# A hybrid decoder layer on one core: the list schedule's reserve for TensorE's operands becomes a preference, and the kept weights get another layout

## The chip, the cores and the metric

The kernel runs on one core of one Trainium2 chip. The metric is the device time of one execution in microseconds. The program is built once by a Python script: the script lists all operations of the layer, a list scheduler in the script decides in which order each engine gets them, and each engine then works through its own queue in that fixed order, waiting on semaphores where an operand is not there yet. The engines are TensorE (PE, with its weight loads PEld), VectorE (DVE), ScalarE (ACT), GpSimd (POOL) and SyncE (SP), which issues nearly all DMAs.

## The reference

One decoder layer for 2048 tokens of width 1024, in float32. An input `x` is normalized and modulated, multiplied by one wide input matrix (columns gq, gk, gv, ga, gz for gated linear attention, sq, sk, sv, sz for sliding window attention), goes through the two kinds of attention, then through one output matrix, and is normalized again:

```python
h = rmsnorm(x, g_norm) * (1 + scale) + shift
proj = einsum('bsd,de->bse', h, w_in)
gq, gk, gv, ga, gz, sq, sk, sv, sz = split_cols(proj, COL_SIZES)
o_gla = rmsnorm(gla_chunked(gq, gk, gv, log_sigmoid(ga @ w_decay + b_decay) / 16), g_head) * silu(gz)
o_swa = sliding_window_sink_attention(rope(sq), rope(sk), sv, sinks) * silu(sz)
x = x + gate * (concat([o_gla, o_swa]) @ w_out)
return rmsnorm(x, g_final)
```

## The kernel before, in words

**Tiling.** The 2048 tokens are four units (`u` = 0 to 3) of 512. For each unit the input product is made slot by slot: a slot is a group of columns (`qk0`, `gz0`, `sz0`, `qk1`, `gz1`, `sz1`, `kv`, `sq`, `gv`). Each float32 operand is split into a high part rounded to a format that TensorE takes in one pass and a low part, the rest. A product is then three: high by high, high by low, low by high (`mm3`). So in the rows `hh`, `hl` are the two parts of the normalized input (eight tiles, one for each 128 of the 1024 rows of the matrix, counted by `k`), and `w_sz`, `w_gz`, `w_kv` and so on hold both parts of a slot's weights.

**Weights.** In unit 0 each raw weight tile (`wr_...`) comes by DMA from the input, ACT rounds it to the high part (CAST), and DVE or POOL subtracts for the low part. Both parts are then stored to a buffer in the chip's memory (`wc`), and units 1 to 3 load them from there. The slots `qk0`, `gz0`, `sz0` of unit 0 are made first, together, `k` by `k`, while the input is still being normalized (`first_w`, `proj_t_outer`; products `po`). Their weights lie in the tiles `first` (qk0) and `own` (gz0 and sz0, one pair for each `k`).

**Buffers.** Weight tiles of all slots share five buffers (`WB`): the two `first` tiles, then `w_sz_0`, `w_gz_0` and `w_kv_0`. The sixth tile, `w_kv_1`, takes the buffer of the first `first` tile, `w_kv_2` that of the second, `w_kv_3` that of `w_sz_0`, and the tiles of the next slot that of `w_gz_0`. A tile can only be written when its buffer's former content has been read by TensorE and stored to `wc`. Products of a slot go to one of two PSUM banks (tag `mm`) and are evacuated by ACT (`zs`, `kvr`); a third product tile needs the first one evacuated. Raw tiles take turns in three buffers (`st`) or four (`wst`); the four lie in memory which the start of unit 0 uses until its last `hl` is made.

**Order.** `Order.issue` holds a model of the engines. At each step it takes the engine that can begin earliest, and on it, among the operations whose operands the model has ready, the one with the lowest key (the program's order, with lifts). For an operation of TensorE an operand counts as ready 0.9 in the model's clock (`SLACK`) after its producer has ended and the semaphore has hopped over: `after()`, line 303. If no operation of TensorE is ready by that measure, the model lets TensorE stand until one is. Nothing of these 0.9 is in the program itself: only the order that comes out is. A store to `wc` has its key raised by 400 or more, so that it comes late on SP.

Of the kernel before, what the change touches and what calls it, by code (L numbers as in the profile page):

```python
# [18 lines left out]
P = 128  # L19
# [76 lines left out]
class Order:  # L96
# [122 lines left out]
    def issue(self):  # L219
# [14 lines left out]
        for g in units:  # L234
            inside = {o.idx for o in g}
            deps = {d for o in g for d in o.deps if d.idx not in inside}
            ready = 0.0
            pending = set()
            for d in deps:
                if d.start is None:  # L240
                    pending.add(unit_of[d.idx])
                else:
                    ready = max(ready, self.after(d, g[0]))
            need[g[0].idx] = [len(pending), ready, g, deps]
            for p in pending:
                users.setdefault(p, []).append(g[0].idx)
# [13 lines left out]
        for k, (n, ready, g, _) in need.items():  # L260
            if n == 0:
                avail[g[0].eng].append([ready, g[0].key, k])
        left = len(units)
        out = []
        while left:
# [36 lines left out]

    def after(self, d, o):
# [89 lines left out]
def layer_kernel(ctx, tc, x, xT, w_ada, w_gate, b_cols, b_gate, g_cols, c_cols, pos, inv_freq,  # L393
# [30 lines left out]
    def f(ap):  # L424
        return ap.bitcast(F32)
# [239 lines left out]
    def first_w():  # L665


        n = SLOT_N["qk0"]
        t0 = [w_tile(f"w{i}_first").rearrange("p (k n) -> p k n", n=n) for i in "hl"]
        t1 = [[hp.tile([P, 2, n], F32R, name=f"w{'hl'[i]}_own{k}", tag="hh" if i == 0 else "hl")  # L670
               if k < KT - 2 else
               near.tile([P, 2, n], F32R, name=f"w{'hl'[i]}_own{k}", tag=f"qk{i}" if k == KT - 2 else "zs",
                         bufs=2 if k == KT - 2 else ZS)
               for k in range(KT)] for i in range(2)]
        src = w_in[:, 0:3 * KT * n].rearrange("p (k n) -> p k n", n=3 * n)
        raws = {}

        def load(k):
            raws[k] = begin.tile([P, 3, n], F32, name=f"wr_first{k}", tag="st0", bufs=3)
            SY.dma_start(raws[k].rearrange("p a b -> p (a b)"), src[:, k])  # L680

        def part(k):
            raw = raws.pop(k)
            both = ([t[:, k] for t in t0], raw[:, 0]), ([t[k] for t in t1], raw[:, 1:3])
            for d, r in both:
                (G.tensor_copy if k == 0 else A.copy)(d[0], r)
            for d, r in both:
                G.tensor_tensor(d[1], r, f(d[0]), ALU.subtract)
            if k == 0:
                for i in range(2):  # L690
                    keep_k(i, 0)

        def keep_k(i, k, lift=None):
            o = 2 * SLOT_O["gz0"]
            to = wc[:, o:o + 4 * KT * n].rearrange("p (s c i k m) -> p s c i k m", s=2, c=2, i=2, k=KT)
            od.lift = LATER if lift is None else lift
            x = SY.dma_start(f(to[:, :, :, i, k]), f(t1[i][k]).rearrange("p s (c m) -> p s c m", c=2))
            od.lift = 0
            return x

        def keep_parts(after):
            ops = [keep_k(i, k, 0) for k in (KT - 1, KT - 2) for i in range(2)]
            o = 2 * SLOT_O["qk0"]
            to = wc[:, o:o + 2 * KT * n].rearrange("p (c i k m) -> p c i k m", c=2, i=2, k=KT)
            for i in range(2):
                for c in range(2):
                    ops.append(SY.dma_start(f(to[:, c, i]), f(t0[i][:, :, c * P:(c + 1) * P])))
            for x in ops:
                x.deps.add(after)

        def keep_rest():
            after = od.ops[-1]
            for i in range(2):
                for k in range(1, KT - 2):
                    keep_k(i, k, 0).deps.add(after)

        parts = [[[t0[i][:, k] for k in range(KT)] for i in range(2)]]
        for j in range(2):
            parts.append([[t1[i][k][:, j] for k in range(KT)] for i in range(2)])
        return parts, load, part, keep_parts, keep_rest  # L720
# [13 lines left out]
    def slot_w(u, name, lift=LIFT):  # L734
# [7 lines left out]
        tiles = {}  # L742
        kept = wc[:, 2 * o:2 * (o + KT * n)].rearrange("p (j i k m) -> p j i k m", j=count, i=2, k=kk)
        src = w_in[:, o:o + KT * n].rearrange("p (j k m) -> p j k m", j=count, k=kk)
        step = max(1, NB // m)

        def load(j):
            t = w_tile(f"w_{name}{u}_{j}")[:, :2 * kk * m].rearrange("p (i k m) -> p i k m", i=2, k=kk)
            tiles[j] = t
            od.lift = -lift  # L750
            if u == 0:
                for k in range(0, kk, step):
# [5 lines left out]
                    raw = raw[:, :step * m].rearrange("p (k m) -> p k m", k=step)  # L758
                    h_, l_ = [t[:, i, k:k + step] for i in range(2)]
                    SY.dma_start(raw, src[:, j, k:k + step])  # L760
# [4 lines left out]
            else:  # L765
                for k in range(0, kk, kk // 2):
                    SY.dma_start(f(t[:, :, k:k + kk // 2]), f(kept[:, j, :, k:k + kk // 2]))

        stream.extend([lambda j=j: load(j) for j in ([int(half)] if half else range(count))])

        def w(i, k, c=0):
            return tiles[k // 2][:, i, k % 2] if wide else tiles[c][:, i, k]

# [169 lines left out]
    def proj_t_outer(ws, each):  # L943
# [5 lines left out]
        for k in range(KT):  # L949
            each(k)  # L950
            for h in halves(k):
                for i, w in enumerate(ws):
                    for ct in range(2):
                        cs = slice(ct * P, (ct + 1) * P)
                        p = ps[2 * i + ct]

                        for n, (a, b) in enumerate(((w[0], hh), (w[1], hh), (w[0], hl))):
                            mmul(p[:, h], a[k][:, cs], b[k][:, h], k == 0 and h.start == 0 and n == 0,
                                 k == KT - 1 and n == 2, p)
# [618 lines left out]
```

## Time and profile before

| | |
|---|---|
| three timed runs | 835.5, 836.94, 837.18 us, median 836.94 |
| profiled execution: device time | 835.71 us |
| profiled execution: span from first to last instruction | 834.0 us |
| TensorE busy | 809.6 us, 97% of the span |
| DVE, ACT, POOL busy | 72%, 61%, 47% |
| granted clock of TensorE, mean | 0.997 |
| DMA | 200.81 MB, 118812 packets, queue of SP 68.8% of 16 engines |

Times in the rows are counted from the start of the span. An idle time stands in square brackets before the instruction that ended it, with the instruction or DMA that released it. A busy TensorE is modelled from the start and size of its products; the distance from one product's start to the next shows the rate at which they really follow each other.

### The profile page before, as it was taken

The numbers are of one execution on the slowest core, as the hardware profiler recorded it, in microseconds if no ns is written. First come the engines' busy times: TensorE is split into PE (matmuls) and PEld (weight loads), VectorE is DVE, ScalarE is ACT, GpSimd is POOL, SyncE is SP. The second block draws the span as 40 slices with busy tenths as digits, with TensorE's granted clock in tenths as the row PEclk, the third lists the DMA queues.
The fourth block names the chain that finished last, engine by engine and source line by source line (L and its number), as shares of the span: only waits on it lengthen the run. The fifth ranks groups of instructions, "written<-read, shape, count | busy, mean of one in ns | idle before, by whom it ended". The sixth has DMA issues, their size and how long they took to land.

```text
span 834.0 us, 13255 instructions
## 1 busy us (share of the span) xinstructions
PE 809.6 (97%) x4274; PEld 671.9 (81%) x4274; DVE 597.4 (72%) x1140; ACT 511.0 (61%) x1271; POOL 396.0 (47%) x461
## 2 busy tenths in 40 slices
PE   7998999999999999999999999999999999999995
PEld 6777788879888787888878888888888888888884
DVE  6986567678568978785797747524675766889895
ACT  4567865898556778675587857524677633344431
POOL 4512225456632558645667544322462514665642
PEclk9999999999999999999999999999999999999998
DMA  9969997847448499598887938637467864454432
GB/s 339 377 196 354 388 357 297 288 150 267 174 169 286 142 370 332 180 327 307 284 296 271 380 117 301 219 111 267 143 209 265 288 216 166 141 162 152 140 101 101
DMA packets 118812, 200.81 MB, mean 241 GB/s; under 512 B 10275, under 2 KB 42070, under 8 KB 116054
## 3 DMA queue, kind: packets, MB, share of 16 engines
q1 hardware_dynamic: 117734, 199.91, 68.8%
q8 instruction: 34, 0.56, 0.3%
q14 instruction: 36, 0.29, 0.1%
q10 hardware_dynamic: 1008, 0.05, 0.1%
HBM read 145.26 MB, written 54.66 MB: 240 GB/s over the span
## 4 chain that ended last, share of the span: by engine, by line
PE 67%; DVE 3%; ACT 2%; DMA 2%; POOL 2%; issue 1%; DVEq 0%; ACTq 0%; POOLq 0%
PE pt L439 18%; PE pn L439 17%; PE ya L439 10%; PE ys L439 9%; PE ppo L439 3%; PE psc L439 2%; PE po L439 2%; DMA xt<-in_xT 1%; PE ppt L444 1%; PE pc L439 1%; DMA xn<-in_x 1%; PE pms L439 1%; PE pu L439 1%; ACT s L387 1%; DVE hl L387 1%
## 5 line engine op out<-in xcount | busy, mean ns | idle before, releaser
L439 PE MATMUL pn<-w_gv,hh 128*128 128x512 f32 x256 | 85.6, 398 | 0.0
L439 PE MATMUL pn<-w_sq,hh 128*128 128x512 f32 x256 | 82.0, 395 | 0.0
L439 PE MATMUL pt<-hh,w_gz 128*128 128x512 f32 x224 | 74.8, 397 | 0.1
L439 PE MATMUL pt<-hh,w_qk 128*128 128x512 f32 x224 | 74.9, 399 | 0.0
L439 PE MATMUL pt<-hh,w_sz 128*128 128x512 f32 x224 | 72.8, 394 | 0.2 <-ACT hh L387 0.2
L387 POOL TENSOR_TENSOR y<-u,y 128x512 f32<-128x512 f32 x28 | 42.4, 1518 | 56.7 <-DVE y L387 33.3
L387 ACT ACTIVATE ge<-ge 128x512 f32<-128x512 f32 x96 | 60.6, 631 | 11.3 <-DVE ge L387 10.0
L387 ACT ACTIVATE s<-s,nm 128x129 f32<-128x129 f32 x128 | 51.4, 402 | 19.5 <-DVE nm L387 18.9
L387 POOL TENSOR_TENSOR xt<-xt,rstd 128x512 f32<-128x512 f32 x27 | 38.5, 1433 | 41.1 <-DMA xt<-in_xT 25.6
L439 PE MATMUL pn<-w_kv,hh 128*128 128x272 f32 x256 | 51.1, 292 | 5.1 <-ACT zs L387 1.8
L439 PEld LDWEIGHTS pn<-w_sq,hh 128*128 128x128 f32 x256 | 47.5, 188 | 10.5 <-issue 0.5
L439 PEld LDWEIGHTS pn<-w_gv,hh 128*128 128x128 f32 x256 | 47.1, 188 | 8.6
L439 PE MATMUL ys<-woht,m 128*128 128x512 f32 x168 | 53.4, 392 | 0.0
L439 PE MATMUL pn<-w_gv,hl 128*128 128x512 f32 x128 | 50.4, 394 | 0.0
L439 PE MATMUL pn<-w_sq,hl 128*128 128x512 f32 x128 | 50.3, 393 | 0.0
L387 POOL TENSOR_TENSOR s<-s,den 128x512 f32<-128x512 f32 x32 | 35.2, 1103 | 30.8 <-DVE den L387 24.1
L439 PE MATMUL ya<-wohb,m 128*128 128x512 f32 x152 | 49.6, 392 | 0.0
L439 PEld LDWEIGHTS pt<-hh,w_sz 128*128 128x128 f32 x224 | 41.9, 188 | 9.1 <-ACT hh L387 0.5
L387 POOL TENSOR_TENSOR o<-o,zs 128x128 f32<-128x128 f32 x64 | 34.4, 558 | 31.0 <-DVE o L387 25.5
L439 PEld LDWEIGHTS pt<-hh,w_gz 128*128 128x128 f32 x224 | 41.6, 188 | 9.0 <-DVE w_gz L387 0.6
L387 ACT CAST m<-mr 128x512 fp32r<-128x512 f32 x39 | 23.1, 618 | 41.9 <-PE ya L439 20.7
L439 PEld LDWEIGHTS pt<-hh,w_qk 128*128 128x128 f32 x224 | 41.6, 188 | 7.9
(272 smaller groups left out, 2388.2 us busy)
## 6 DMA issues: line engine op xcount, KB each, us to landing
w_sz<-wc SPq DMA_DIRECT2D x24, 512.0 KB, 6.4
w_sq<-wc SPq DMA_DIRECT2D x24, 512.0 KB, 7.6
w_qk<-wc SPq DMA_DIRECT2D x24, 512.0 KB, 7.0
w_gv<-wc SPq DMA_DIRECT2D x24, 512.0 KB, 8.6
w_gz<-wc SPq DMA_DIRECT2D x24, 512.0 KB, 6.5
mr<-mixd SPq DMA_DIRECT2D x32, 256.0 KB, 3.0
y<-in_x SPq DMA_DIRECT2D x32, 256.0 KB, 3.4
out<-y SPq DMA_DIRECT2D x32, 256.0 KB, 2.2
```

Source lines behind the costliest of these rows:

```text
L387: return order.add(eng, lambda: real(*args, **kw), dur, ins, outs, lock=lock, nbytes=nbytes)
L439: return od.add("PE", lambda: T.matmul(o, l, r, start=start, stop=stop), dur, [l, r] + ([] if start else [o]), [bank if start and bank is ...
L444: return od.add("PE", lambda: T.transpose(o, i, ident), 0.109, [i, ident], [o], mode="few" if o.shape[0] <= 32 else None)
```

## The change

Two edits are made. The first is in the scheduler: for an operation of TensorE an operand now counts as ready as soon as its producer has ended and the hop is over (`HARD` = 0). The old measure with 0.9 added is kept as a second number, `soft`. Among the operations that are ready, the model picks by key among those whose `soft` time has passed; if there are none, it takes the one whose `soft` time comes first. So TensorE never stands in the model while anything can begin.

The second is the layout of the weights in their tiles and in `wc`. Before, all high parts of a tile came first and then all low parts; now high and low alternate for each 128 (or, in wide slots, 272 or 512) columns. A reload of half a tile is then one run of 4096 bytes a partition (`kv`: 2176) where it was two of 2048 (1088). The `own` tiles hold one slot each with both parts, stored in runs of 1024 bytes (512 before); a `first` tile holds both parts of four `k`, stored in runs of 4096 (512 before). To fill them, ACT's and POOL's operations on each raw tile of `first_w` become three of 256 columns each where there were two, of 256 and 512.

```diff
+HARD = 0.0
+WEIGH = 0.0
...
-            pick = min((x for x in lst if when(x, e) <= t + 1e-9), key=lambda x: x[1])
+            now = [x for x in lst if when(x, e) <= t + 1e-9]
+            safe = [x for x in now if x[3] <= t + 1e-9]
+            pick = min(safe, key=lambda x: x[1]) if safe else min(now, key=lambda x: (x[3] + WEIGH * x[1], x[1]))
...
                     ready = max(self.after(d, first) for d in x[3])
-                    avail[first.eng].append([max(ready, x[1]), first.key, u])
+                    soft = max(self.after(d, first, True) for d in x[3])
+                    avail[first.eng].append([ready, first.key, u, soft])
...
-        return d.end + HOP[o.eng] + (SLACK if o.eng == "PE" else SPARE if d.eng == "G" else 0.0) + (PATIENT if o.late and d.bytes else 0.0)
+        t = d.end + HOP[o.eng] + (PATIENT if o.late and d.bytes else 0.0)
+        if o.eng == "PE":
+            return t + (SLACK if soft else HARD)
+        return t + (SPARE if d.eng == "G" else 0.0)
...
         def part(k):
             raw = raws.pop(k)
-            both = ([t[:, k] for t in t0], raw[:, 0]), ([t[k] for t in t1], raw[:, 1:3])
-            for d, r in both:
-                (G.tensor_copy if k == 0 else A.copy)(d[0], r)
-            for d, r in both:
-                G.tensor_tensor(d[1], r, f(d[0]), ALU.subtract)
+            homes = [t0[k // half][:, :, k % half]] + t1[k]
+            for j, t in enumerate(homes):
+                (G.tensor_copy if k == 0 else A.copy)(t[:, :, 0], raw[:, j])
+            for j, t in enumerate(homes):
+                G.tensor_tensor(t[:, :, 1], raw[:, j], f(t[:, :, 0]), ALU.subtract)
...
-                    ops.append(SY.dma_start(f(to[:, c, i]), f(t0[i][:, :, c * P:(c + 1) * P])))
+                    ops.append(SY.dma_start(f(kept(0)[:, c, i * half:(i + 1) * half]), f(t0[i][:, c])))
...
-            t = w_tile(f"w_{name}{u}_{j}")[:, :2 * kk * m].rearrange("p (i k m) -> p i k m", i=2, k=kk)
+            t = w_tile(f"w_{name}{u}_{j}")[:, :2 * kk * m].rearrange("p (k i m) -> p k i m", i=2, k=kk)
...
-                    SY.dma_start(f(t[:, :, k:k + kk // 2]), f(kept[:, j, :, k:k + kk // 2]))
+                    SY.dma_start(f(t[:, k:k + kk // 2]), f(kept[:, j, k:k + kk // 2]))
```

On TensorE the order differs, against the kernel before, from the start to 234 us of the old trace and from 350 to 490 us; elsewhere it is the same. The number of products is the same.

**First place: SP's queue in unit 0, where the weights of slot `kv` are fetched.** Before, behind the first two stores of `own` tiles (the second half of `w_gz_0`, `wr_gz_04`, follows much later, behind the stores of the `first` tiles):

```order
L387 DMA wr_gz_00_187<-in_w_in 128x512
L387 DMA wc<-wh_own_129 128x4x128
L387 DMA wc<-wl_own_137 128x4x128
L387 DMA wr_kv_00_201<-in_w_in 128x272
L387 DMA wr_kv_01_202<-in_w_in 128x272
L387 DMA wr_kv_10_204<-in_w_in 128x272
L387 DMA wr_kv_30_231<-in_w_in 128x272
...
L387 DMA wc<-wl_first 128x8x128 x2
L387 DMA wr_gz_04_188<-in_w_in 128x512
L387 DMA wc<-w_sz_0_183 128x2048
```

Now:

```order
L389 DMA wr_gz_00_187<-in_w_in 128x512
L389 DMA wc<-w_own_129 128x2x256
L389 DMA wc<-w_own_130 128x2x256
L389 DMA wr_gz_04_188<-in_w_in 128x512
L389 DMA wr_kv_11_205<-in_w_in 128x272
L389 DMA wc<-w_sz_0_183 128x2048
...
L389 DMA wr_kv_00_201<-in_w_in 128x272
L389 DMA wr_kv_01_202<-in_w_in 128x272
...
L389 DMA wc<-w_first_127 128x1024 x2
L389 DMA wc<-w_first_128 128x1024
```

The second half of `gz` and the store of `w_sz_0` have moved from behind the stores of the `first` tiles to ahead of them, and ahead of the loads into `w_kv_0`.

**Second place: ACT's queue at the same point of the program.** `zs<-pt_229` and `zs<-pt_235` empty the PSUM banks of the slots `sz1` and `gz1`; the casts make the high parts of the `kv` weights. Before:

```order
L387 CAST w_kv_1_203<-wr_kv_10_204 128x272
L387 CAST w_kv_1_203<-wr_kv_11_205 128x272
L387 COPY zs<-pt_229 128x512
L387 ACTIVATE ge<-ge 128x512
L387 CAST w_kv_2_206<-wr_kv_20_207 128x272
L387 CAST w_gz_0_186<-wr_gz_04_188 128x512
L387 ACTIVATE ge<-ge 128x512 x3
L387 CAST w_kv_3_230<-wr_kv_30_231 128x272
L387 CAST w_kv_3_230<-wr_kv_31_232 128x272
L387 COPY zs<-pt_235 128x512
```

Now:

```order
L389 CAST w_kv_3_230<-wr_kv_30_231 128x272
L389 COPY zs<-pt_229 128x512
L389 ACTIVATE ge<-ge 128x512
L389 CAST w_kv_1_203<-wr_kv_10_204 128x272
L389 CAST w_kv_1_203<-wr_kv_11_205 128x272
L389 ACTIVATE ge<-ge 128x512
L389 CAST w_kv_3_230<-wr_kv_31_232 128x272
L389 ACTIVATE ge<-ge 128x512 x2
L389 COPY zs<-pt_235 128x512
L389 CAST w_kv_2_206<-wr_kv_20_207 128x272
L389 CAST w_kv_2_206<-wr_kv_21_208 128x272
```

`zs<-pt_229` no longer stands behind the casts into `w_kv_1`, only behind one into `w_kv_3`; the casts into `w_kv_2` now stand behind `zs<-pt_235`.

**Third place: TensorE's queue at the same point.** `pt_235` is the product of the second half-slot of `gz1`, `pn_241` and `pn_246` are the first two token tiles of `kv`. Before, twelve of the twenty-four products of `pt_235` were followed by `kv`:

```order
L439 MATMUL pt_235<-hh_3_165,w_gz_0_186 128x512
L439 MATMUL pn_241<-w_kv_0_200,hh_0_153 128x272 x2
L439 MATMUL pn_241<-w_kv_0_200,hl_0_154 128x272
...
L439 MATMUL pn_241<-w_kv_2_206,hl_4_170 128x272
L439 MATMUL pt_235<-hh_4_169,w_gz_0_186 128x512
L439 MATMUL pt_235<-hl_4_170,w_gz_0_186 128x512
```

Now all of `pt_235` comes first, and the parts of `pn_241` and `pn_246` that need only `w_kv_0` and `w_kv_1` stand ahead of any that needs `w_kv_2`:

```order
L441 MATMUL pt_235<-hh_7_181,w_gz_0_186 128x512
L441 MATMUL pn_241<-w_kv_0_200,hh_0_153 128x272 x2
...
L441 MATMUL pn_241<-w_kv_1_203,hl_3_166 128x272
L441 MATMUL pn_246<-w_kv_0_200,hh_0_153 128x272 x2
...
L441 MATMUL pn_246<-w_kv_1_203,hh_2_161 128x272
L441 MATMUL pn_241<-w_kv_2_206,hh_4_169 128x272
```

Nineteen products of `kv` (12 of `pn_241`, 7 of `pn_246`) now stand between the end of `gz1`'s half and the first that needs `w_kv_2`; before, twelve stood there (those of `pn_241` on `w_kv_0` and `w_kv_1`).

## Rows read from the trace of the kernel before

**Rows 1.** The page's first part: busy time, share of the span and instructions of each engine.

```profile
PE 809.6 (97%) x4274; PEld 671.9 (81%) x4274; DVE 597.4 (72%) x1140; ACT 511.0 (61%) x1271; POOL 396.0 (47%) x461
```

**Rows 2.** Stretches of the span: length, busy time and instructions of each engine, granted clock, DMA share, GB/s.

```profile
0.00:20.00 20.00, 16.39 (x102) 14.05 (x102) 12.57 (x27) 9.62 (x19) 7.79 (x18) 1.00 0.90 335
20.00:58.60 38.60, 36.34 (x164) 29.64 (x163) 36.93 (x57) 23.74 (x51) 17.20 (x20) 1.00 0.81 283
58.60:83.00 24.40, 19.61 (x122) 16.61 (x122) 16.21 (x40) 17.40 (x35) 5.43 (x11) 1.00 1.02 352
83.00:130.00 47.00, 46.81 (x250) 38.23 (x249) 26.54 (x55) 33.55 (x71) 12.35 (x24) 1.00 1.02 378
130.00:234.00 104.00, 102.14 (x576) 85.59 (x575) 76.70 (x168) 78.97 (x220) 60.83 (x84) 1.00 0.62 216
...
350.00:430.00 80.00, 78.23 (x461) 66.23 (x461) 58.56 (x115) 53.14 (x126) 41.87 (x51) 1.00 0.88 310
430.00:490.00 60.00, 60.00 (x311) 49.58 (x310) 44.58 (x86) 46.26 (x131) 40.90 (x49) 1.00 0.79 279
```

**Rows 3.** Waits of TensorE over the whole span: who waited for whom, us in total, times, longest.

```profile
PE ppo L439 <- POOL pp L387: 0.9, 3, 0.5
...
PE pn L439 <- DMA w_kv<-wc: 0.4, 1, 0.4
```

**Rows 4.** TensorE in order of time, from 58 to 83 us: start, length, instruction, count, idle time before it and its releaser.

```profile
58.66 0.39 PE L439 MATMUL pt<-hh,w_gz 128*128 128x512 f32 x1
...
61.15 0.39 PE L439 MATMUL pt<-hh,w_gz 128*128 128x512 f32 x1
62.70 0.52 PE L439 MATMUL pn<-w_kv,hh 128*128 128x272 f32 x2 [1.16 <-ACT zs L387]
...
65.40 0.87 PE L439 MATMUL pn<-w_kv,hh 128*128 128x272 f32 x2 [0.93 <-ACT w_kv L387]
...
70.31 0.52 PE L439 MATMUL pn<-w_kv,hh 128*128 128x272 f32 x2 [0.68 <-ACT zs L387]
...
72.21 0.40 PE L439 MATMUL pn<-w_kv,hh 128*128 128x272 f32 x1 [0.62 <-ACT w_kv L387]
...
76.90 0.52 PE L439 MATMUL pn<-w_kv,hh 128*128 128x272 f32 x2 [1.19 <-ACT kvr L387]
...
77.38 0.41 PE L439 MATMUL pn<-w_kv,hh 128*128 128x272 f32 x2
...
82.61 0.41 PE L439 MATMUL pn<-w_kv,hh 128*128 128x272 f32 x2
...
82.98 0.38 PE L444 MATMUL pkr<-ident,kr 128*128 128x128 f32 x2
```

**Rows 5.** ACT in the same stretch, same columns.

```profile
61.43 0.74 ACT L387 CAST w_kv<-wr_kv 128x272 fp32r<-128x272 f32 x2 [1.88 <-DMA wc<-wh_first]
62.07 0.58 ACT L387 COPY zs<-pt 128x512 f32<-128x512 f32 x1
...
64.93 0.42 ACT L387 CAST w_kv<-wr_kv 128x272 fp32r<-128x272 f32 x1 [1.74 <-DMA wc<-wl_first]
...
68.73 0.74 ACT L387 CAST w_kv<-wr_kv 128x272 fp32r<-128x272 f32 x2 [0.70 <-DMA wc<-w_sz]
...
72.70 1.28 ACT L387 ACT_TABLE_LOAD   x1
...
76.47 0.39 ACT L387 COPY kvr<-pn 128x272 f32<-128x272 f32 x1
```

**Rows 6.** SP's DMA issues from 30 to 63 us: start, time spent on the issue, instruction, count.

```profile
36.80 0.97 SPq L387 DMA_DIRECT2D wc<-wl_own  x1
48.35 1.78 SPq L387 DMA_DIRECT2D wr_kv<-in_w_in  x4
...
57.38 3.08 SPq L387 DMA_DIRECT2D wc<-wl_first  x2
60.50 1.29 SPq L387 DMA_DIRECT2D wr_gz<-in_w_in  x1
```

**Rows 7.** Three short stretches in the columns of rows 2: SP's queue blocked; the stores of the `first` tiles in runs of 512 bytes; loads and stores in runs of 2 KB and more.

```profile
42.00:48.00 6.00, 6.00 (x27) 4.92 (x27) 4.99 (x9) 5.05 (x11) 3.10 (x3) 1.00 0.03 8
...
59.00:63.00 4.00, 2.84 (x14) 2.07 (x13) 2.30 (x5) 2.12 (x5) 0.00 (x0) 1.00 1.12 342
...
68.00:72.00 4.00, 2.91 (x16) 2.06 (x14) 2.68 (x6) 2.26 (x6) 1.39 (x1) 1.00 1.06 417
```

**Rows 8.** The instructions on the raw tiles of `kv`, last line of the view: time from a load's issue to its landing.

```profile
DMA to landing us min/median/max: 2.1/2.5/4.4
```

**Rows 9.** ACT near the start, columns of rows 4: the chain to the first input tile, and the casts of one raw tile of `first_w`.

```profile
13.19 0.69 ACT L387 ACTIVATE rstd<-ss,eps_c 128x512 f32<-128x512 f32 x1 [0.62 <-PE ss L439]
...
14.45 0.58 ACT L387 ACTIVATE ss<-rstd 128x512 f32<-128x512 f32 x1
...
24.10 0.39 ACT L387 CAST wh_first<-wr_first 128x256 fp32r<-128x256 f32 x1
24.40 0.62 ACT L387 CAST wh_own<-wr_first 128x512 fp32r<-128x512 f32 x1
```

**Rows 10.** POOL's two subtractions for the same raw tile, columns of rows 4.

```profile
24.57 0.75 POOL L387 TENSOR_TENSOR wl_first<-wr_first,wh_first 128x256 fp32r<-128x256 f32 x1 [1.68 <-ACT wh_first L387]
25.27 1.32 POOL L387 TENSOR_TENSOR wl_own<-wr_first,wh_own 128x512 fp32r<-128x512 f32 x1
```

More of the change, by code (lines that the diff above doesn't have):

```diff
@@ L236, in issue @@
             deps = {d for o in g for d in o.deps if d.idx not in inside}
[L237 to L244, printed above, removed]
+            pending = {unit_of[d.idx] for d in deps if d.start is None}
+            need[g[0].idx] = [len(pending), 0.0, g, deps]
             for p in pending:
@@ L261, in issue @@
             if n == 0:
-                avail[g[0].eng].append([ready, g[0].key, k])
+                avail[g[0].eng].append([0.0, g[0].key, k, 0.0])
         left = len(units)
@@ L668, in first_w, with own @@
         n = SLOT_N["qk0"]
[L669 to L674, printed above, removed]
+        half = KT // 2
+        t0 = [w_tile(f"w_first{i}").rearrange("p (c k i m) -> p c k i m", c=2, k=half, i=2) for i in range(2)]
+        def own(k, j):
+            name = f"w_own{k}{j}"
+            if k < KT - 2:
+                t = hp.tile([P, NB], F32R, name=name, tag="hh" if j == 0 else "hl")
+            elif k == KT - 2:
+                t = near.tile([P, NB], F32R, name=name, tag=f"qk{j}", bufs=2)
+            else:
+                t = near.tile([P, NB], F32R, name=name, tag="zs", bufs=ZS)
+            return t.rearrange("p (c i m) -> p c i m", c=2, i=2)
+        t1 = [[own(k, j) for j in range(2)] for k in range(KT)]
         src = w_in[:, 0:3 * KT * n].rearrange("p (k n) -> p k n", n=3 * n)
@@ L712, in keep_rest @@
             after = od.ops[-1]
-            for i in range(2):
+            for j in range(2):
                 for k in range(1, KT - 2):
-                    keep_k(i, k, 0).deps.add(after)
-        parts = [[[t0[i][:, k] for k in range(KT)] for i in range(2)]]
+                    keep_k(j, k, 0).deps.add(after)
+        parts = [[[[t0[k // half][:, c, k % half, i] for c in range(2)] for k in range(KT)] for i in range(2)]]
         for j in range(2):
-            parts.append([[t1[i][k][:, j] for k in range(KT)] for i in range(2)])
+            parts.append([[[t1[k][j][:, c, i] for c in range(2)] for k in range(KT)] for i in range(2)])
         return parts, load, part, keep_parts, keep_rest
@@ L742, in slot_w @@
         tiles = {}
-        kept = wc[:, 2 * o:2 * (o + KT * n)].rearrange("p (j i k m) -> p j i k m", j=count, i=2, k=kk)
+        kept = wc[:, 2 * o:2 * (o + KT * n)].rearrange("p (j k i m) -> p j k i m", j=count, i=2, k=kk)
         src = w_in[:, o:o + KT * n].rearrange("p (j k m) -> p j k m", j=count, k=kk)
@@ L758, in load @@
                     raw = raw[:, :step * m].rearrange("p (k m) -> p k m", k=step)
-                    h_, l_ = [t[:, i, k:k + step] for i in range(2)]
+                    h_, l_ = [t[:, k:k + step, i] for i in range(2)]
                     SY.dma_start(raw, src[:, j, k:k + step])
@@ L953, in proj_t_outer @@
                     for ct in range(2):
-                        cs = slice(ct * P, (ct + 1) * P)
                         p = ps[2 * i + ct]
                         for n, (a, b) in enumerate(((w[0], hh), (w[1], hh), (w[0], hl))):
-                            mmul(p[:, h], a[k][:, cs], b[k][:, h], k == 0 and h.start == 0 and n == 0,
+                            mmul(p[:, h], a[k][ct], b[k][:, h], k == 0 and h.start == 0 and n == 0,
                                  k == KT - 1 and n == 2, p)
```

25 lines of the change are left out of this document (12 added, 13 removed).

## The prediction

> **What bounds the kernel now.** I read the page's busy times first: TensorE works in 97% of the span [rows 1], so the time is its work plus the time in which it stands. The number of products does not change; only its idle time can. Second, the stretches of the span, which tell where it stands [rows 2]: the difference between length and busy time is 3.61 us up to 20 us, 2.26 up to 58.6, 4.79 from 58.6 to 83, 0.19 up to 130, 1.86 up to 234, 1.77 between 350 and 430, and nothing from 430 to 490. The stretches in which the order stays as it was (234 to 350, and from 490 on) keep their times, merely shifted. Third, TensorE and ACT in order of time in the worst stretch [rows 4, 5], and SP's queue, which feeds it [rows 6].
>
> What the reader is to see there: at 62.70 TensorE waits 1.16 us "for ACT zs", the emptying of a PSUM bank. ACT did that at 62.07, only behind two casts of `kv` weights which themselves waited 1.88 us for the store of a `first` tile [rows 5]. The casts write the buffer that this store has to empty. At 64.93 it happens again with the second `first` tile, at 68.73 with `w_sz`. So the root is SP's queue. It stood from 37.77 (36.80 + 0.97) to 48.35 behind a load of `kv` whose buffer was not free [rows 6], with the DMA engines at 3% [rows 7], and then had everything to move at once, at a DMA share of 1.02 [rows 2].
>
> How much is lost there: `gz` products follow each other in (61.15 − 58.66)/11 = 0.226 us, `kv` products in (82.61 − 77.38)/42 = 0.1245 us (14 groups of three) [rows 4]. The stretch from 58.66 to 82.98 holds 24 of the first and 96 of the second, 5.43 + 11.95 = 17.38 us of work; it took 24.32. Lost: 6.94 us, of which 4.79 show as idle time and the rest as slow restarts.
>
> **The change, part by part.** *The weights of unit 0.* SP now issues the second half of `gz` and the store of `w_sz_0` ahead of the loads into `w_kv_0`, instead of at 60.50 and after [rows 6]. TensorE can then run all 24 `gz` products from 58.66 to 58.66 + 5.43 = 64.09. The bank of `sz1` is emptied behind one cast into `w_kv_3`, whose buffer was stored early, and not behind the store of a `first` tile; so the waits of 1.16 at 62.70 and 0.68 at 70.31 have no cause left. After 64.09 come 19 `kv` products that need only `w_kv_0` and `w_kv_1`, 2.37 us: `w_kv_2` is wanted at 66.46.
>
> When can it be there? Its buffer is free when the last `first` store has landed. From `wr_gz_04` to that store SP issues 0.26 MB (gz), 8 × 0.139 = 1.11 (`kv` loads), 1.05 (`w_sz_0`), 1.05 (four `own`), 2.10 (four `first`) and 0.26 (sz), 5.83 MB in all. The DMA engines moved 342 GB/s while they wrote runs of 512 bytes and 417 with longer ones [rows 7]; I take 380, the middle. From 48.4, when SP got free before, that is 15.3 us. A load of 0.139 MB, 0.4 us of transfer, took 2.1 at the least from issue to landing [rows 8], so 1.7 us come on top: 65.4. Two casts (0.74 [rows 5]) and a subtraction as long as half of that make 66.5: `w_kv_2` is just in time. At 342 GB/s it is 1.8 us late; I count half of that, 0.9. Behind it the casts of the next weights and the table load of 1.28 us still stand in ACT's queue near a bank's evacuation [rows 5], though two evacuations are now ahead of the load: of the 1.19 us at 76.90 I keep 0.7. So 6.94 − 1.6 = 5.3 us go. Bounds: all of it, 6.9; or only the two waits on `zs`, 1.16 + 0.68 = 1.8.
>
> What is late next: the `gv` weights, wanted 5.3 us earlier. In the old trace the whole stretch to 130 has a DMA share of 1.02 and TensorE stands 0.19 us in it [rows 2]; ahead of the last `gv` load SP now has one store of 1.05 MB less (2.8 us at 380 GB/s), and 3.7 MB of `own` and `first` stores go in longer runs (10.8 us at 342, 8.9 at 417). Together that is 4.7 us of the 5.3. I put it at nothing lost, and at 5.3 − 4.7 = 0.6 in the bad case, which the bounds above cover.
>
> *Longer runs by themselves.* At a full DMA share the stretch of 512-byte stores moved 342 GB/s and the one of longer runs 417 [rows 7]; that is in the sum above. In units 1 to 3 the reloads can gain only in landing time, and TensorE waited for one only once, 0.4 us [rows 3]: 0 to −0.4, I take 0. The Trainium skill, "DMA: Bandwidth & Descriptors", section Specifications, gives 512 bytes as the smallest transfer that runs at line rate; by it the new stores would be no faster than the old ones, and the time that of the first rival below. The two stretches do not bear it out.
>
> *The start.* ACT's exponential (`ss<-rstd`) began at 14.45, behind `amul`, though its operand ended at 13.19 + 0.69 = 13.88 [rows 9]; the new order puts it ahead of `amul`, behind an operation of 0.3: −0.3, which the later wait for the second input tile can swallow. Against it, casts of 512 columns become two of 256: 2 × 0.39 − 0.62 = 0.16 us for seven raw tiles on ACT [rows 9], and 2 × 0.75 − 1.32 = 0.18 for eight on POOL [rows 10]. They lie beside 18 products a tile, 18 × 0.226 = 4.1 us, which need 3 × 0.75 = 2.3 us of POOL. If that cover failed at the last tile, where the new order also puts three casts of `sz` and `gz` ahead of the input tile, it would cost about 0.6. I take 0; bounds −0.3 to +0.6.
>
> *The order from 130 to 234 and 350 to 490.* The reserve kept a product from being queued close behind its producer; as a preference it does so only where other work is ready. Idle time there is 1.86 + 1.77 = 3.63 us, and another order loses some of these waits and makes others: 0 net. From 430 to 490 there is nothing to win, so a new order can only lose; I take half of what the other two stretches show, 0.9. Bounds: −1.8 (half the waits go) and +4 (the sum of idle time doubles).
>
> *Sum.* −5.3 + 0 + 0 + 0.9 = −4.4. The profiled execution took 835.71 us, 834.0 of span and 1.71 around it; 4.4 less is 831.3. It lies 1.23 below the median of the timed runs, 836.94; on the median's scale the forecast is 832.5 us.
>
> **The rivals.**
>
> *The stores still set the pace.* If the stores gain nothing from longer runs, or if SP's queue blocks as long behind `wr_gz_04` as it did behind `wr_kv_00`, the `first` stores end no earlier and every tile behind them is as late. Then only the two `zs` waits go, −1.8, and +0.9 from the later order stays: 836.94 − 0.9 = 836.0. For it: the hole of 42 to 48 us [rows 7] comes from a buffer set free at 48, and the new head of the queue waits for work of the same time. Against it: 342 against 417 GB/s.
>
> *Slower: products without reserve in the sliding window attention.* Where no other product is ready, the new rule queues attention products right behind their producers on ACT and POOL, and TensorE, strictly in order, stands in front of ready work when one is late. The nearest row is a wait of 0.3 us each (0.9 in three, [rows 3]). With the 5.3 us won in unit 0 it is slower from (5.3 + 1.7)/0.3 = 24 new waits on; the order differs in about 40 places behind 130 us. With 30 waits it is 9 − 5.3 = +3.7: 840.6. Against it: in these stretches TensorE has long slots of input products at hand as a filler.
>
> *Better.* All 6.9 us of the stretch go, and half of the 3.63 us later: 836.94 − 6.9 − 1.8 = 828.2. For it: the new queue order removes the causes and not only the waits.
>
> **How the numbers follow.** The forecast has 0.60, the pacing stores 0.15, slower attention 0.12, better 0.13. A measurement of this kernel can tell 0.2%, 1.7 us, from no change: faster means below 835.2. Faster holds the better case and nearly all of the forecast's (0.57), 0.71 with a little of the pacing case; the same is most of the pacing case and a tail of the forecast's, 0.16; slower 0.13. The forecast's own range is 829.5 to 835. The range for 8 in 10 goes from 828.5, near the better case, to 837.0, past the pacing case, and leaves out the attention case and the end of the better one.
>
> **What would show it.** In the new profile: the stretch from the first `gz` product of `pt_235` to the last of `kv` takes 17.4 + 1.6 us and TensorE's waits on ACT `zs` and `w_kv` there are gone; `gz`'s second half is issued around 49 us; ACT's casts into `w_kv_1` no longer wait for a `first` store past 62 us; the first `gv` product stands about 5 us earlier than before. The stretches 234 to 350 and 490 to the end have their old lengths. It is wrong if ACT's casts into `w_kv_2` or the next `sz` weights wait for stores beyond 67 us, if the `gv` products start with a wait of more than 1 us, or if the idle time behind 130 us rises by more than 2 us.

## The result and the profile after

| | before | after |
|---|---|---|
| median of four runs | 837.06 us (835.5 to 837.7) | 828.88 us (828.45 to 829.23) |
| profiled execution: device time, span | 835.71, 834.0 | 829.2, 827.5 |

The ratio is 0.9909 [0.9894, 0.9923]: 8.2 us faster. A second series gave 829.0 against 836.05, ratio 0.9911 [0.9892, 0.9930], some 7 us, which is nearer to the 6.5 of the two profiled executions. Both intervals leave out 1.

The page of the changed kernel, answering to [rows 1]: TensorE's work is the same, the span is shorter.

```profile
PE 808.5 (98%) x4274; PEld 671.8 (81%) x4274; DVE 596.9 (72%) x1140; ACT 510.6 (62%) x1278; POOL 396.2 (48%) x470
```

The stretches in the columns of [rows 2]:

```profile
0.00:20.00 20.00, 16.32 (x102) 13.86 (x102) 11.86 (x26) 9.81 (x20) 7.14 (x19) 1.00 0.89 331
20.00:58.60 38.60, 36.39 (x164) 30.13 (x165) 36.25 (x58) 24.81 (x58) 20.69 (x28) 1.00 0.86 315
58.60:83.00 24.40, 23.11 (x144) 20.59 (x143) 19.51 (x47) 20.83 (x45) 5.23 (x10) 1.00 1.01 368
83.00:130.00 47.00, 46.74 (x246) 37.78 (x245) 28.50 (x58) 31.36 (x64) 16.08 (x27) 1.00 0.99 383
130.00:234.00 104.00, 102.88 (x585) 86.52 (x583) 75.83 (x162) 79.78 (x220) 59.30 (x84) 1.00 0.57 200
...
350.00:430.00 80.00, 79.55 (x445) 66.75 (x444) 58.52 (x122) 55.18 (x133) 46.32 (x55) 1.00 0.84 308
430.00:490.00 60.00, 58.97 (x317) 48.28 (x316) 43.81 (x86) 41.41 (x118) 35.30 (x46) 1.00 0.74 254
```

From 58.6 to 83 us TensorE is now idle for 1.29 us and not 4.79; 144 products stand there, not 122. Behind 130 us the idle time falls from 1.86 to 1.12 and from 1.77 to 0.45, and between 430 and 490 it rises from nothing to 1.03 (these stretches are cut by time, and the products of the changed kernel stand some 6 us earlier in them).

TensorE in the worst stretch, columns of [rows 4]:

```profile
58.22 0.39 PE L441 MATMUL pt<-hh,w_gz 128*128 128x512 f32 x1
...
63.44 0.39 PE L441 MATMUL pt<-hh,w_gz 128*128 128x512 f32 x1
65.67 0.52 PE L441 MATMUL pn<-w_kv,hh 128*128 128x272 f32 x2 [0.35 <-ACT zs L389]
71.09 0.52 PE L441 MATMUL pn<-w_kv,hh 128*128 128x272 f32 x2 [0.62 <-ACT kvr L389]
...
77.08 0.29 PE L441 MATMUL pn<-w_kv,hl 128*128 128x272 f32 x1
77.69 0.50 PE L441 MATMUL pt<-hh,w_sz 128*128 128x512 f32 x1 [0.32 <-ACT kvr L389]
...
83.90 0.73 PE L441 MATMUL pn<-w_gv,hh 128*128 128x512 f32 x2 [0.22 <-ACT kvr L389]
```

All `gz` products run at once, and no wait for weights is left. The waits of 1.16 and 0.68 for `zs` are one of 0.35. SP's queue, which answers to [rows 6]:

```profile
46.51 0.34 SPq L389 DMA_DIRECT2D wr_gz<-in_w_in  x1
...
47.45 0.43 SPq L389 DMA_DIRECT2D wc<-w_sz  x1
...
55.53 2.16 SPq L389 DMA_DIRECT2D wc<-w_first  x3
...
60.27 0.60 SPq L389 DMA_DIRECT2D wc<-w_first  x1
```

The second half of `gz` is issued at 46.51, before at 60.50. SP still stands ahead of it: its issue before that, of two stores of `own` tiles, ended at 37.81, so the queue is blocked for 8.7 us where it was blocked for 10.6. ACT, answering to [rows 5]:

```profile
61.31 0.74 ACT L389 CAST w_kv<-wr_kv 128x272 fp32r<-128x272 f32 x2 [0.38 <-DMA wc<-w_first]
...
65.05 0.57 ACT L389 COPY zs<-pt 128x512 f32<-128x512 f32 x1
65.52 0.74 ACT L389 CAST w_kv<-wr_kv 128x272 fp32r<-128x272 f32 x2
```

ACT waits 0.38 us for the store of a `first` tile, where it waited 1.88 and 1.74; the casts into `w_kv_2` at 65.52 wait for no DMA.

### The profile page after: what moved, and what is told of

Same layout as the page of the kernel before. It is cut to its first block, busy times and chain, and to the rows that moved or that the text cites. A ratio compares the mean times of both kernels' runs of the same rounds, so it can differ in the third digit from the quotient of the medians.

```text
span 827.5 us, 13273 instructions
## 1 busy us (share of the span) xinstructions
PE 808.5 (98%) x4274; PEld 671.8 (81%) x4274; DVE 596.9 (72%) x1140; ACT 510.6 (62%) x1278; POOL 396.2 (48%) x470
## 4 chain that ended last, share of the span: by engine, by line
PE 74%; ACT 6%; DVE 5%; DMA 5%; issue 2%; POOL 2%; SPq 0%; DVEq 0%; ACTq 0%; POOLq 0%
PE pn L441 21%; PE pt L441 20%; PE ya L441 10%; PE ys L441 9%; PE ppo L441 3%; PE psc L441 3%; PE po L441 2%; DMA xt<-in_xT 2%; PE ppt L446 1%; ACT s L389 1%; PE pc L441 1%; DMA xn<-in_x 1%; PE pms L441 1%; PE pu L441 1%; DMA wc<-w_kv 1%
## 5 line engine op out<-in xcount | busy, mean ns | idle before, releaser
L389 ACT CAST m<-mr 128x512 fp32r<-128x512 f32 x39 | 23.1, 617 | 40.2 <-PE ya L441 20.5
```

Source lines behind the costliest of these rows:

```text
L389: return order.add(eng, lambda: real(*args, **kw), dur, ins, outs, lock=lock, nbytes=nbytes)
```

## The experiments

Three theories were set against each other for unit 0. RULE: the preference brings the gain. QUEUE: the gain is the order of SP's queue. RUNS: the longer runs of the stores free the buffers earlier. For the products behind 130 us there were two. PREFERENCE: picking a safe product among the ready ones saves time. CHANCE: every new order makes some waits and loses others, and this one is a good draw.

The table cuts each profiled execution at products that all kernels share (starts, in us): the first `gz` product of `pt_235`, the last `kv` product of unit 0, and the first `gv` product. Ratios are to the kernel before in the same series: 837.06 for the row "after", 836.2 for e1 to e4, 836.05 for e5 to e8 and 835.89 for e9 to e12 (4, 23, 19 and 15 runs). The rows "after" and e5 are one program; their difference shows how far a single profile can be trusted: 0.6 us in the stretch, 1.2 at the first `gv`, 0.7 behind it.

| kernel | first gz | gz to last kv | first gv | gv to end of span | median | ratio |
|---|---|---|---|---|---|---|
| before | 58.66 | 24.19 | 88.67 | 745.3 | | 1 |
| after | 58.22 | 18.86 | 83.90 | 743.6 | 828.88 | 0.9909 |
| e5, after again | 57.79 | 18.26 | 82.72 | 744.3 | 829.00 | 0.9911 [0.9892, 0.9930] |
| e1, old layout, preference 0.9 | 60.90 | 23.77 | 90.38 | 745.6 | 841.57 | 1.0066 [1.0046, 1.0086] |
| e9, e1 again | 60.06 | 26.71 | 92.49 | 747.5 | 841.69 | one run |
| e11, old layout, preference 1.2 | 58.56 | 28.90 | 93.16 | 750.2 | 842.97 | 1.0086 [1.0061, 1.0110] |
| e3, old layout, wait 1.2 | 59.59 | 21.52 | 86.94 | 747.0 | 835.27 | 0.9989 [0.9976, 1.0001] |
| e2, new layout, wait 0.9 | 57.40 | 19.86 | 83.11 | 748.3 | 833.12 | 0.9964 [0.9951, 0.9977] |
| e10, new layout, wait 1.2 | 57.00 | 21.22 | 84.04 | 752.1 | 837.04 | 1.0009 [0.9994, 1.0024] |
| e4, after, short runs | 57.62 | 19.94 | 84.23 | 745.7 | 831.18 | 0.9941 [0.9928, 0.9954] |
| e6, after, reserve 0 | 57.89 | 18.19 | 82.80 | 756.8 | 841.54 | 1.0064 [1.0040, 1.0088] |
| e7, after, reserve 0.6 | 57.41 | 17.79 | 82.61 | 752.1 | 836.46 | 1.0009 [0.9994, 1.0024] |
| e8, after, reserve 1.2 | 57.37 | 17.98 | 82.03 | 748.0 | 831.59 | 0.9944 [0.9926, 0.9962] |
| e12, after, 1.2 up to 100 us | 57.91 | 17.98 | 82.58 | 741.9 | 828.00 | 0.9909 [0.9894, 0.9924] |

### The two edits apart: e1, e9, e2

e1 and e9 are the kernel before with the whole edit of the scheduler and nothing else; its core:

```diff
+HARD = 0.0
...
+            safe = [x for x in now if x[3] <= t + 1e-9]
+            pick = min(safe, key=lambda x: x[1]) if safe else min(now, key=lambda x: (x[3] + WEIGH * x[1], x[1]))
```

e2, against the changed kernel:

```diff
-HARD = 0.0
+HARD = 0.9
```

> The kernel before with the scheduler's edit alone (old layout of the weights). In its plan SP's queue in unit 0 stays word for word as it was (the second half of gz behind the stores of the first tiles); on ACT only zs<-pt_229 moves ahead of the two casts into w_kv_1. Theory RULE (the preference brings the gain): 6 to 8 us faster than before, near 829 to 831. Theory QUEUE (the gain is the order of SP's queue in unit 0, which the new layout alone brings into the plan): the stretch from the first gz product to the last of kv stays 23 to 24.5 us long, only the wait of 1.16 us at 62.7 goes; with the later order, which the rule does change, 0 to 3 us faster, 834 to 837. Theory RUNS (the longer runs of the stores free the buffers earlier): the same as QUEUE here.

> The changed kernel with HARD = 0.9, so that the reserve is a wait again, and the new layout kept. SP's queue in unit 0 is nearly that of the changed kernel. RULE: within 1 us of the kernel before, 836 to 837.5. QUEUE and RUNS: the stretch from the first gz product to the last of kv takes 19 to 20.5 us as in the changed kernel, and the first waits are 0.4 us shorter: 4 to 6 us faster than before, 831 to 833; what is left to 828.9 belongs to the rule in the later order.

RULE falls: alone, the rule makes the kernel 5.4 us slower, and the layout alone makes it 3.1 us faster with a stretch of 19.86. The new queue on SP is in e2's plan and not in e1's. ACT's `zs` stands ahead of the two casts in e1's plan too, and the wait of 1.16 us at 62.70 is gone there, but the stretch is only 0.4 us shorter (23.77): that part of the new order alone brings little. Yet e1 was slower than any theory said, and its profile is of the fastest of its six executions. e9 is the same program once more.

> The kernel before with the scheduler's edit alone once more, for a second profile: the first was of its fastest execution (837.8, against a median of 841.6). If its loss is a fall of TensorE's granted clock in the start, this profile shows 0.5 somewhere before 60 us or at another wait, and the products behind it 3 to 6 us later than in the kernel before; if it is a sum of small waits, the granted clock stays at 1.0 and the distance to the kernel before grows by steps of under 1 us.

The first answer holds up to the first `gv` product, which is 3.8 us late. Another 2.2 us come behind it, where the clock stays at 1.00 up to the last products and the longest wait is 1.26 us: that part is nearer to the second answer. In e9 the granted clock falls at two places. TensorE at the second, and then the stretches there:

```profile
79.28 0.53 PE L441 MATMUL pn<-w_kv,hh 128*128 128x272 f32 x2 [2.10 <-ACT kvr L389]
```

```profile
78.00:80.00 2.00, 0.72 (x4) 0.72 (x5) 1.54 (x4) 2.00 (x7) 0.52 (x1) 0.91 0.75 290
80.00:82.00 2.00, 2.00 (x11) 2.00 (x10) 1.64 (x7) 1.37 (x3) 1.78 (x4) 0.50 0.97 272
82.00:84.00 2.00, 2.00 (x14) 2.00 (x13) 0.88 (x3) 0.00 (x0) 1.06 (x3) 0.73 1.05 385
84.00:86.00 2.00, 2.00 (x18) 2.00 (x17) 1.27 (x4) 1.80 (x5) 0.32 (x1) 1.00 1.06 436
```

Behind a wait of 2.10 us the clock stands at 0.50, the lower of its two levels (1.2 GHz), and only 11 products start in two microseconds where 18 do later. In e1, the same program, the same wait took 2.12 us and the clock stayed at 1.00:

```profile
80.00:82.00 2.00, 2.00 (x18) 2.00 (x18) 1.64 (x5) 0.84 (x2) 1.88 (x4) 1.00 1.00 252
82.00:84.00 2.00, 2.00 (x18) 2.00 (x18) 1.71 (x7) 1.90 (x5) 0.89 (x3) 1.00 0.90 336
```

25 products in these 4 us and 36: 11 at 0.1245, some 1.4 of the 2.9 us by which the two stretches differ (26.71 and 23.77). In the start both executions lose: behind waits of 1.1 to 1.5 us near 21 to 24 us the clock is at 0.50 (for some 7 us in e1, 3 in e9), and the first `gz` comes at 60.90 and 60.06 and not at 58.66. In the kernel before waits of the same length stand there (1.03, 0.77 and 1.49) and the clock stays at 1.00. The other executions agree: the mean granted clock is 0.991 to 0.994 in e1's six and 0.994 to 0.998 in the 23 of the kernel before. The averages differ by 0.0038, which makes an estimate of 3.2 us of the 5.4.

### Queue against runs: e3 and e4

e3 is the kernel before with another reserve; in its plan SP's queue turns into the new one, with the old layout.

```diff
-SLACK = 0.9
+SLACK = 1.2
```

> The kernel before with SLACK = 1.2 and nothing else: old layout, stores in runs of 512 bytes, the reserve still a wait and a longer one. In its plan the second half of gz and the store of w_sz_0 stand ahead of the kv loads on SP, as in the changed kernel. QUEUE: the stretch from the first gz product to the last of kv falls from 24.3 to 19.5 to 21.5 us, and the time by 3 to 5 us, 832 to 834, if the later order costs nothing. RUNS: the casts into w_kv_2 wait for the 512-byte stores, the stretch stays above 22.5 us, at most 2 us are won, 835 or more. RULE: a longer reserve loses, 837 or more.

The stretch is 21.52: between the two, since both are at work. The plan with the new queue brings 2.7 us; the casts still wait for the stores in 512-byte runs, as ACT shows:

```profile
64.57 0.74 ACT L387 CAST w_kv<-wr_kv 128x272 fp32r<-128x272 f32 x2 [0.74 <-DMA wc<-wh_first]
...
67.63 0.74 ACT L387 CAST w_kv<-wr_kv 128x272 fp32r<-128x272 f32 x2 [1.78 <-DMA wc<-wl_first]
```

Its time misses the expected 832 to 834, for the start and the later order lose 0.9 and 1.6 us.

e4 keeps the changed kernel's plan and shortens the runs of the stores alone; its core:

```diff
-t0 = [w_tile(f"w_first{i}").rearrange("p (c k i m) -> p c k i m", c=2, k=half, i=2) for i in range(2)]
+t0 = [w_tile(f"w_first{i}").rearrange("p (k i c m) -> p c k i m", c=2, k=half, i=2) for i in range(2)]
...
-            return t.rearrange("p (c i m) -> p c i m", c=2, i=2)
+            return t.rearrange("p (s c m) -> p s c m", s=2, c=2)
```

> The changed kernel with the own tiles holding one part of both slots again and the first tiles holding their columns crosswise, so that all their stores are written in runs of 512 bytes instead of 1024 and 4096; the plan of every engine is the changed kernel's, step for step, and the reloads of units 1 to 3 are too. QUEUE: 0 to +1.0 us against the changed kernel (the stores of 5.8 MB before the last first store take at most 1 to 2 us longer, and TensorE wants w_kv_2 only after 19 products), 829 to 830. RUNS: casts into w_kv_1 and w_kv_2 end 1.5 to 3 us later and TensorE waits for w_kv_2 about 65 to 68 us, +2 to +4, 831 to 833.

+2.2 us by the medians of e4 and e5: the number of RUNS, though not at the place that RUNS named, since TensorE has no wait for `w_kv_2`. The same stretches of time, of e4 and then of the changed kernel:

```profile
54.00:60.00 6.00, 6.00 (x28) 4.99 (x27) 5.11 (x10) 3.61 (x8) 0.00 (x0) 1.00 1.00 294
60.00:66.00 6.00, 4.72 (x27) 3.95 (x25) 4.70 (x10) 3.03 (x8) 0.00 (x0) 1.00 1.04 304
```

```profile
54.00:60.00 6.00, 6.00 (x28) 4.99 (x27) 4.76 (x10) 3.29 (x8) 0.00 (x0) 1.00 0.98 337
60.00:66.00 6.00, 5.65 (x31) 4.77 (x30) 5.35 (x13) 4.63 (x11) 0.77 (x1) 1.00 1.04 393
```

At nearly the same DMA share (last but one column) the engines move 294 and 304 GB/s with the short runs among their transfers, 337 and 393 with the long ones. e4's last `first` store is issued at 61.89, though its SP got free 0.64 us earlier than in the changed kernel (45.87 against 46.51), where it is issued at 60.27. TensorE pays at one place, where ACT's `zs` (at 65.94) stands behind a cast that waits for such a store, and behind one that waits for a load which SP issues after those stores. ACT, then TensorE:

```profile
61.71 0.74 ACT L389 CAST w_kv<-wr_kv 128x272 fp32r<-128x272 f32 x2 [1.59 <-DMA wc<-w_first]
...
64.43 0.42 ACT L389 CAST w_kv<-wr_kv 128x272 fp32r<-128x272 f32 x1 [0.41 <-DMA wr_kv<-in_w_in]
```

```profile
66.57 0.52 PE L441 MATMUL pn<-w_kv,hh 128*128 128x272 f32 x2 [1.85 <-ACT zs L389]
```

So of the 5.3 us by which the stretch got shorter, the new plan with short runs brings 4.25 (24.19 to 19.94), and the runs 1.1, or 1.7 against e5. The new plan changes SP's, ACT's and TensorE's order together, and which of them brings how much was not separated: e3, with the new queue, short runs and other orders of casts and products, gets 2.7. Another 1.4 to 2.1 lie behind the first `gv`, in part at 153 us, where TensorE waits 1.35 us for POOL, which got an input tile late. Why that load landed late, and whether the short runs are the cause, is not shown. POOL of e4, then of the changed kernel:

```profile
151.03 1.29 POOL L389 TENSOR_TENSOR xt<-xt,rstd 128x512 f32<-128x512 f32 x1 [6.05 <-DMA xt<-in_xT]
```

```profile
149.19 1.30 POOL L389 TENSOR_TENSOR xt<-xt,rstd 128x512 f32<-128x512 f32 x1 [4.76 <-DVE den L389]
```

e4 has `own` tiles as in the kernel before and still the new queue. With the new layout it is therefore not the new `own` tiles that turn the queue in the plan; whether it is the `first` tiles of four `k` or the three operations a raw tile was not tried. Nor is the new layout needed for it: e3 has the new queue with the old layout and a longer wait.

### The reserve and the later order: e5 to e8, e10 to e12

e5 is the changed kernel word for word. e6, e7 and e8 change one line of it (below, e7; 0 and 1.2 in the others), e10 has 1.2 for both numbers of e2, e11 1.2 for the one of e1:

```diff
-SLACK = 0.9
+SLACK = 0.6
```

e12, against the changed kernel:

```diff
+SLACK = 0.9; EARLY, UNTIL = 1.2, 100
...
-            return t + (SLACK if soft else HARD)
+            return t + ((EARLY if t < UNTIL else SLACK) if soft else HARD)
```

> The changed kernel once more, word for word, so that the next three stand beside it on the same chip: 828 to 830 us by every theory.

> The changed kernel with SLACK = 0: no reserve at all, neither as a wait nor as a preference; unit 0's queue on SP as in the changed kernel. Theory PREFERENCE (picking the safe product among the ready ones is what saves time behind 130 us): the waits of TensorE on ACT, DVE and POOL behind 130 us rise from about 4 us to 7 or more, 832 to 835. Theory CHANCE (every new order of the products makes and loses some waits, and the changed kernel has drawn a good one): between 829 and 835, with no tie to the size of the reserve; its stretch from the first gz product to the last of kv stays at 19 to 20.5 us.

> The changed kernel with the preferred reserve at 0.6 instead of 0.9, nothing else. PREFERENCE: the number of unsafe picks hardly changes, so within 1.5 us of the changed kernel, 828 to 830.5. CHANCE: anywhere between 829 and 835, most likely slower than the changed kernel by 1 to 4 us, with one or two waits of over 1 us at places where the changed kernel has none.

> The changed kernel with the preferred reserve at 1.2 instead of 0.9, nothing else. PREFERENCE: as with 0.6, within 1.5 us of the changed kernel, 828 to 830.5. CHANCE: anywhere between 829 and 835, most likely slower than the changed kernel by 1 to 4 us.

PREFERENCE is refuted by e7: a reserve of 0.6 for 0.9 costs 7.5 us. CHANCE fits better, but its range of 829 to 835 was too narrow for e6 and e7. Against e5 the three stand at the first `gv` product between 0.1 us later and 0.7 earlier, which is within the difference of two executions, and behind it they lose 3.7 to 12.5. Four values of the reserve cannot tell a draw from a best value near 0.9: in the part behind `gv` 0, 0.6 and 0.9 come in falling order (756.8, 752.1, 744.3). e7's loss is one wait; TensorE, then the stretches:

```profile
362.87 1.11 PE L446 MATMUL pk<-ident,qk 128*128 128x128 f32 x4 [5.35 <-DVE qk L389]
```

```profile
362.00:364.00 2.00, 1.11 (x4) 0.71 (x4) 1.09 (x4) 1.94 (x4) 0.60 (x2) 0.50 1.02 395
364.00:366.00 2.00, 1.93 (x5) 1.49 (x5) 1.44 (x3) 0.80 (x3) 1.55 (x2) 0.50 1.01 410
366.00:368.00 2.00, 2.00 (x18) 1.46 (x16) 0.00 (x0) 0.88 (x3) 0.00 (x0) 0.55 1.06 385
```

DVE ended the operand of `pk` 5.35 us later than TensorE came to it. No reserve of 0.6 or 0.9 covers that. The products of `sz` behind `pk` could not have filled the time either, as ACT, DVE and TensorE's weight loads show:

```profile
355.96 0.63 ACT L389 ACTIVATE xn<-xn 128x512 f32<-128x512 f32 x1 [2.62 <-DMA xn<-in_x]
...
363.65 0.37 ACT L389 COPY kvr<-pn 128x272 f32<-128x272 f32 x1
```

```profile
361.41 0.17 DVE L389 COPY elast<-ep 128x4 f32<-128x4 f32 x1 [0.87 <-ACT ep L389]
```

```profile
364.07 0.29 PEld L441 LDWEIGHTS pt<-hh,w_sz 128*128 128x128 f32 x1 [0.48 <-ACT kvr L389]
```

The first `sz` product waits for `kvr`, the emptying of its PSUM bank, which ACT ended at 364.02. DVE waited for ACT as well, and ACT had stood 4.2 us in three waits for loads of `xn` (2.62, 0.37 and 1.21). So ACT is late for both, and the loads stand at the head of the chain; why they landed late was not followed. e2 has a long wait too, on `dgh`:

```profile
398.42 0.50 PE L441 MATMUL pr<-dgh,ones_r 128*128 128x512 f32 x1 [2.69 <-DVE dgh L389]
...
400.47 0.63 PE L441 MATMUL pn<-w_sq,hh 128*128 128x512 f32 x1
400.89 0.63 PE L441 MATMUL pr<-dgl,ones_r 128*128 128x512 f32 x1
401.32 0.63 PE L441 MATMUL pn<-w_sq,hh 128*128 128x512 f32 x1
```

Behind it products of 512 columns start every 0.43 us, where 0.23 is normal, until the clock is back at about 402.8. Twelve products stand between 398.42 and 402.84, 4.42 us where 12 × 0.23 = 2.76 would do: 1.7 us on top of the 2.69. In e8 two waits (1.23 and 2.02, on DVE `o` and `Q`, at 342 to 346) have the same effect:

```profile
342.55 1.13 PE L441 MATMUL po<-sT,v 128*128 128x128 f32 x8 [1.23 <-DVE o L389]
345.70 2.07 PE L441 MATMUL po<-sT,v 128*128 128x128 f32 x8 [2.02 <-DVE Q L389]
```

The same two waits, 1.2 to 1.5 and 2.0 us with the clock at 0.50 around them, stand in all four kernels with 1.2 throughout (e3, e8, e10, e11), whatever their layout and rule, and in none with 0.9. So this loss goes with the size of the reserve in these kernels and is not mere chance, against CHANCE as it was put. e6 has no wait over 2.1 us behind 130 us and no fall of the clock ahead of its last products; its 12 us behind `gv` come in many steps, TensorE's busy time is 7 us longer, and their causes were not followed up.

> The new layout with the reserve as a wait (HARD = SLACK = 1.2). PREFERENCE: slower than the same reserve as a preference (831.6), 833 to 836. CHANCE: anywhere between 829 and 836; what decides is whether a single wait of over 2 us behind 130 us is in its order. By both the stretch from the first gz product to the last of kv takes 19 to 20.5 us, since the new queue on SP is in its plan.

> The old layout with the preference at 1.2 instead of 0.9 (HARD = 0). Its plan keeps SP's old queue in unit 0, so by QUEUE the stretch from the first gz product to the last of kv stays at 23 to 24.5 us and the time at 834 to 842. PREFERENCE: faster than the kernel before with a wait of 1.2 (835.3) although the queue is the old one, 831 to 834. CHANCE: 834 to 842.

e10's 837.04 lies above both ranges. Its stretch is 21.22 and not 20.5 at most, for a wait of 2.58 on `kvr` stands in it, and at 352.77 TensorE waits 2.03 for DVE `Q`. e11's 842.97 lies 1 us above the range of CHANCE, and its stretch is 28.90 where 24.5 was the most that was expected: waits of 2.28 for `w_kv` and 2.11 for `kvr` stand in it, and behind each the clock is at 0.50 for some 3 us. With the new layout the preference beats the wait at both reserves (829.0 against 833.1, 831.6 against 837.0); with the old one it loses at both (841.6 against 836.2, 843.0 against 835.3). By itself neither rule is the better one. Nor do the two edits add up: the layout alone gives −3.1, the rule alone +5.4, both together −7 to −8.

> The changed kernel with the preferred reserve at 1.2 for operands that are ready before 100 us of the model's clock, and 0.9 behind: TensorE's order changes up to the first gv products, and from about 110 us on it is the changed kernel's, row for row. In the profile of the kernel with 1.2 everywhere, TensorE stood 0.4 us better than the changed kernel at 58 us and 0.7 us better at 106 us. If these places add up as single terms, 0.4 to 1.0 us faster than the changed kernel, 828.0 to 828.6; if the later waits are only met earlier, the same as the changed kernel.

828.0, as expected, and 1.0 below e5; but the ratios (0.9909 and 0.9911) can't be told apart. That it beats the changed kernel is not shown.

## Why the prediction was right, and where not

The forecast was 832.5. The measured 828.88 lies in the range for 8 in 10, 0.4 above its lower end; it is 3.6 below the forecast and below the forecast's own range of 829.5 to 835. The mechanism and the size of the main term, the weights of unit 0, were right; the term for the later order was wrong.

*The weights of unit 0.* Predicted −5.3 and a stretch of 17.4 + 1.6; measured 24.19 to 18.86, −5.33, and −5.93 in e5. `gz`'s second half at 46.51 (predicted 49), no wait for weights, the first `gv` 4.8 us earlier (predicted 5). `w_kv_2` was wanted at 66.46 and expected at 66.5; its casts stand at 65.52 and wait for no store. The 1.6 that were kept were split wrongly: the 0.9 for `w_kv_2` did not come, the waits on evacuations (0.35 and 0.62) and slow restarts did. That the `gv` weights lose nothing holds: TensorE waits there for `kvr` (0.32 and 0.22), not for weights; with the restarts this gives back 1.0 between the last `kv` and the first `gv`.

*Longer runs by themselves*, 0 to −0.4 beside the sum above: too small, but for another reason than reloads. e4 puts the runs at 2.2 to 2.7 us, of which 1.1 to 1.7 were in the first term. The part behind the first `gv`, 1.4 to 2.1 of it, is measured but not explained. The measured rates differ (294 and 304 GB/s against 337 and 393), and the rival that rested on equal rates (836.0) is out. But its mechanism is real: in e4 late stores still set the pace at 66.57. The Trainium skill, "DMA: Bandwidth & Descriptors", section Specifications, lets transfers of 512 bytes run at line rate. The rates of e4 do not agree with that.

*The start*, 0 with −0.3 as the lower bound: −0.44, and −0.87 in e5. The mechanism came as described: ACT's exponential begins at 14.04 and not at 14.45. The later wait did not swallow it, and the bound was too tight.

*The order from 130 to 234 and 350 to 490*, +0.9 with −1.8 to +4: −1.7 and −1.0 from the first `gv` to the end. This term failed in sign and in its bound: other orders of the same products took up to 13 us more there (e6). That a new order gains as much as it loses does not describe the draws: in every kernel with another plan there than the changed kernel's, the part behind the first `gv` took longer than before, by 0.3 (e1) to 11.5 us (e6). With the changed kernel's plan it took 1.0 to 3.4 less, and 0.3 more in e4. That this draw was a good one is luck as far as the prediction goes; no row of before told it. The slower rival had its price wrong in part: in e2, e7, e8 and e10 what makes a draw bad is not 24 waits of 0.3 us but one of 2 to 5, and the fall of the clock with it. In e6, the slowest of them, it is many small steps, as that rival had it.

*The sum.* Predicted −4.4 on the profiled pair, measured −6.5: −0.44 − 5.33 + 1.0 − 1.7. Most of the remaining distance is the 1.23 us added for the profiled execution of before: in the later series its median lies at 835.9 to 836.2, only 0.2 to 0.5 above that execution. The time came out near the better rival's 828.2, by one of its two terms: −1.7 in the later order for its −1.8, but 5.3 and not 6.9 us in the stretch.

*What the prediction took as one.* It gave the new queue on SP to the change as a whole. At the reserve of 0.9 it comes with the layout, under either rule (e2), and the rule alone does not bring it and loses (e1). A wait of 1.2 brings it with the old layout as well (e3).

## What to carry to other kernels

Where a scheduler's model orders the work, a change of layout can move a whole queue, and a change of rule is one draw among many: compare several settings, and cut the span at shared products before crediting the rule. In a list order look first for the longest single wait of TensorE, and then for what else was late behind it before calling the work behind it ready; in e7 the chain led back to loads that ACT waited for. A larger reserve did not cover such places here (1.2 made one). When a buffer is freed by a store, its run length is a term of the wait.

## What the runs showed of the hardware

A wait of TensorE can cost well over its own length: in e2 the 2.69 us are followed by 1.7 us of lost rate, since the granted clock stands at 0.50 there. Such a stretch at 0.50 lasted some 3 to 7 us (3.3 in e2 and e9, 7 in e1, e7, e8 and e10). The clock fell in or behind waits of 1.24 (e10, at 182.93), 2.10 (e9), 2.11 and 2.28 (e11), 2.69 (e2) and 5.35 (e7), and did not behind 2.06 (e6), 2.12 (e1), 2.58 (e10, at 72.22) and 2.99 (e11, at 324.64): no length decides, and one program differs from run to run, as e1 and e9 show at one and the same wait. In the changed kernel the longest wait between the first and the last products of the layer is 1.57 us, and the clock does not fall between them; its mean is 0.997 to 0.998 in all ten executions.

The spread of a kernel's executions does not tell whether its clock falls: e1's six spread by 5.9 us at a mean clock of 0.991 to 0.994, the six of e5 by 3.7 at 0.997 to 0.998, and the 15 of the kernel before beside e9 to e12 by 5.9 at 0.994 to 0.998.

With stores in runs of 512 bytes among the transfers, the DMA engines moved less at nearly the same busy share: 294 and 304 GB/s against 337 and 393 (e4 and the changed kernel, 54 to 66 us).
